# A decoder block on one core: gate and up by seven block products, their result through DRAM, down for eight output tiles at a time

## The chip, the cores and the metric

The kernel runs on one core of a Trainium2 chip. The metric is the device time of one execution in microseconds. Three runs of the kernel before took 2851.36 to 2853.41 us, with a median of 2852.76.

## The reference, cut to what matters

One hybrid block on 512 tokens of width 2048, in float32: an RWKV-7 branch and a spatial gating branch, merged by gates, an output projection with a residual add, then a SwiGLU channel mixer of hidden width 5632, and a final norm. The change lies in the channel mixer and the output projection ahead of it:

```
    h = h + merged @ w_out[l]
    n = _rmsnorm(h, norm_ffn_g[l])
    h = h + (jax.nn.silu(n @ w_ffn_gate[l]) * (n @ w_ffn_up[l])) @ w_ffn_down[l]
    return _rmsnorm(h, norm_final_g)
```

## The kernel before, in words

Everything is held transposed: a tile has 128 channels on its partitions and the 512 tokens beside each other. 2048 channels are 16 tiles (`KT`), the hidden width is 44 (`NHID`). The factor of the norm (`rs`, one number per token) is applied after the product, its gain before it.

**A product in three matmuls.** Each operand is split into a rounded part (`hi`, type float32r) and the rest (`lo`). `mm3` (L115 to L118) multiplies hi by hi, hi by lo and lo by hi into the same PSUM bank. Weights are the stationary operand, so each matmul comes with a weight load (LDWEIGHTS, engine PEld in the trace). `chunk` (L101 to L109) loads 512 KB of weights on SP's queue, ACT casts them to hi (L96), DVE subtracts to get lo (L99); three buffers of each stand in the pool `wp`. `block` (L133 to L138) computes two output tiles of 128 channels into the two banks of one of two `big` buffers.

**The stages.** Input projections with `nT` as moving tiles, kept in 32 tiles named "a" (L176 to L532); the RWKV chain beside them; the spatial gating (tiles "yb") and the two projections of the branches (tiles "yb" and "ya", L618 to L631), whose result `mg` takes the tiles "a" again; the output projection (L649 to L657), which adds the residual, multiplies by the gain g2 and splits into `n2`, in the tiles "a" too. The output projection's 16 tiles of `h` stay in `hA`.

**Gate, up and down.** `hidden` (L661 to L675) takes hidden tiles one by one: one `block` gives gate and up (2 x 16 x 3 = 96 matmuls of 512 columns), then DVE, ACT (silu), POOL and DVE build the hidden tile, and its two parts go into tiles "at". `down` (L677 to L682) multiplies a group of hidden tiles by their weights and adds to `hA`. The groups have 14, 14, 8, 4 and 4 tiles (L27); the last group's down is done for one half of the tokens and then for the other (`down_sq`, L700), 256 columns a matmul, with the final norm (`rms`, L155) and the stores between.

**Order.** The program is traced once and ordered by a planner, by priorities: what stands under `tc.high_priority()` (weight chunks, drains of PSUM) comes before what else is ready. Every engine then runs its list in that order, and so does SP's queue of DMAs.

**Where tiles lie.** Pools stack up from the left and from the right end of the 128-partition memory. The left one begins with 16 KB of DMA scratch and 8.3 KB of constants, so `wp` starts at byte 24704 of each partition and "a" behind it at 61568, both multiples of 128. The right end is 229344, 96 past a multiple of 128: "yb" and "ya" lie 96 past, the tiles "at", behind smaller ones of `fin`, 32 past.

## Time and profile before

| | |
|---|---|
| median of three runs | 2852.76 us |
| the profiled execution | 2852.42 us |
| its span, first to last instruction | 2850.7 us |
| granted TensorE clock over the span | 0.994 |
| PE busy, matmuls | 98%, 13968 |
| DVE busy | 48% |
| ACT busy | 29% |
| POOL busy | 8% |
| DMA, mean over the span | 121 GB/s |

PE is the matmul engine, PEld its weight loads, which overlap the matmuls; DVE, ACT and POOL work element by element, SP issues the DMAs. A matmul's recorded time includes the way through the array, so neighbours overlap, and the distance between starts tells its price. "Idle before" is the time in which an engine stood still ahead of an instruction, with what ended it.

### The profile page before, as it was taken

How to read it: one execution, taken by the hardware profiler on the slowest of the kernel's cores; microseconds unless marked ns; L12 is line 12 of the kernel's file. 1: busy time of each engine (PE TensorE's matmuls, PEld its weight loads, DVE VectorE, ACT ScalarE, POOL GpSimd, SP SyncE). 2: the span in 40 equal slices, each digit the busy share in tenths (PEclk: the TensorE clock that was granted, in tenths of full speed). 3: DMA queues.
4: the chain of work that ended last, by engine and by line, in shares of the span. 5: the costliest groups of instructions: out<-in, count | busy, mean ns of one | idle time of the engine just before them, and what ended most of it. 6: DMA issues, size and time to landing. Idle time of an engine off the chain costs nothing.

```text
span 2850.7 us, 33823 instructions
## 1 busy us (share of the span) xinstructions
PE 2795.5 (98%) x13968; PEld 2309.3 (81%) x13968; DVE 1359.1 (48%) x1508; ACT 832.5 (29%) x1050; POOL 230.0 (8%) x208
## 2 busy tenths in 40 slices
...
GB/s 161 123 150 155 155 193 117 103 109 104 252 213 120 173 123 136 143 153 96 96 96 96 96 96 89 103 96 96 96 96 90 95 103 97 90 99 98 98 92 152
DMA packets 172729, 345.94 MB, mean 121 GB/s; under 512 B 54304, under 2 KB 91168, under 8 KB 170272
## 3 DMA queue, kind: packets, MB, share of 16 engines
...
q8 instruction: 109, 1.79, 0.3%
...
HBM read 303.90 MB, written 39.85 MB: 121 GB/s over the span
## 4 chain that ended last, share of the span: by engine, by line
PE 85%; DVE 8%; issue 3%; DMA 2%; POOL 1%; SPq 0%; ACT 0%; POOLq 0%; DVEq 0%; ACTq 0%
PE ps_big L118 26%; PE ps_big L117 26%; PE ps_big L116 26%; DVE tmp L394 3%; DVE w_lo L99 2%; DVE X L396 2%; PE ps_big L528 1%; PE ps_big L527 1%; PE ps_big L526 1%; PE rkps L365 1%; DVE gt L512 0%; PE rkps L460 0%; POOL acc L646 0%; PE rkps L499 0%; DMA Ld<-d_l 0%
## 5 line engine op out<-in xcount | busy, mean ns | idle before, releaser
L118 PE MATMUL ps_big<-a,w_lo 128*128 128x512 f32 (+1 forms) x2752 | 1079.8, 393 | 28.0 <-DVE w_lo L99 27.9
L116 PE MATMUL ps_big<-a,w_hi 128*128 128x512 f32 (+1 forms) x2752 | 1077.3, 392 | 5.7 <-ACT w_hi L96 5.7
L117 PE MATMUL ps_big<-a,w_hi 128*128 128x512 f32 (+1 forms) x2752 | 1076.6, 391 | 0.0
L99 DVE TENSOR_TENSOR w_lo<-w_raw,w_hi 128x1024 fp32r<-128x1024 f32 (+2 forms) x500 | 608.9, 1219 | 929.0 <-ACT w_hi L96 924.0
L96 ACT CAST w_hi<-w_raw 128x1024 fp32r<-128x1024 f32 (+2 forms) x500 | 514.1, 1030 | 1497.0 <-PE ps_big L117 1441.6
L118 PEld LDWEIGHTS ps_big<-a,w_lo 128*128 128x128 f32 (+1 forms) x2752 | 518.5, 188 | 148.1 <-DVE w_lo L99 38.9
L116 PEld LDWEIGHTS ps_big<-a,w_hi 128*128 128x128 f32 (+1 forms) x2752 | 518.2, 188 | 114.8 <-ACT w_hi L96 5.7
L117 PEld LDWEIGHTS ps_big<-a,w_hi 128*128 128x128 f32 (+1 forms) x2752 | 518.4, 188 | 110.1 <-issue 0.2
L116 PE MATMUL ps_big<-at,w_hi 128*128 128x512 f32 (+1 forms) x768 | 288.6, 376 | 3.4 <-DVE hA L682 2.3
L118 PE MATMUL ps_big<-at,w_lo 128*128 128x512 f32 (+1 forms) x768 | 288.7, 376 | 0.0
L117 PE MATMUL ps_big<-at,w_hi 128*128 128x512 f32 (+1 forms) x768 | 288.4, 376 | 0.0
L668 POOL TENSOR_TENSOR sl<-sl,rs 128x512 f32<-128x512 f32 x44 | 78.5, 1785 | 1282.0 <-ACT sl L667 1282.0
L116 PEld LDWEIGHTS ps_big<-at,w_hi 128*128 128x128 f32 x768 | 144.0, 188 | 33.2 <-issue 2.5
L117 PEld LDWEIGHTS ps_big<-at,w_hi 128*128 128x128 f32 x768 | 144.0, 188 | 29.4
L118 PEld LDWEIGHTS ps_big<-at,w_lo 128*128 128x128 f32 x768 | 144.0, 188 | 29.3
L394 DVE TENSOR_TENSOR tmp<-X,Ld 128x1 f32<-128x1 f32 (+46 forms) x94 | 141.5, 1505 | 6.3 <-DMA Ld<-d_l 4.0
L666 DVE TENSOR_TENSOR sl<-ps_big,rs 128x512 f32<-128x512 f32 x44 | 30.4, 692 | 145.9 <-PE ps_big L118 145.9
L682 DVE TENSOR_TENSOR hA<-ps_big,hA 128x512 f32<-128x512 f32 (+1 forms) x96 | 53.3, 597 | 74.4 <-PE ps_big L118 74.4
L396 DVE TENSOR_REDUCE X<-tmp 128x1 f32<-128x1 f32 (+46 forms) x94 | 86.8, 923 | 2.3
L646 POOL TENSOR_TENSOR acc<-acc,sq 128x256 f32<-128x256 f32 (+1 forms) x41 | 52.1, 1271 | 433.4 <-ACT sq L645 385.4
L528 PE MATMUL ps_big<-w_hi,a 128*128 128x256 f32 x256 | 73.4, 287 | 0.0
L527 PE MATMUL ps_big<-w_lo,a 128*128 128x256 f32 x256 | 73.3, 286 | 0.0
...
## 6 DMA issues: line engine op xcount, KB each, us to landing
w_raw<-w_gu SPq DMA_DIRECT2D x176, 512.0 KB, 3.7
w_raw<-w_in SPq DMA_DIRECT2D x145, 512.0 KB, 3.7
w_raw<-w_dn SPq DMA_DIRECT2D x88, 512.0 KB, 3.6
...
w_raw<-w_out SPq DMA_DIRECT2D x32, 512.0 KB, 3.7
w_raw<-w_ps SPq DMA_DIRECT2D x16, 512.0 KB, 4.0
w_raw<-w_pr SPq DMA_DIRECT2D x16, 512.0 KB, 3.7
...
```

The source lines that it names most:

```text
L96: act.copy(out=dst, in_=src)
L99: (eng or dve).tensor_tensor(out=dst, in0=src, in1=hi.bitcast(F32), op=ALU.subtract)
L116: pe.matmul(out, wh, xh, start=start, stop=False)
L117: pe.matmul(out, wh, xl, start=False, stop=False)
L118: pe.matmul(out, wl, xh, start=False, stop=stop)
L394: dve.tensor_tensor(out=tv_, in0=X[:, s0:s1, s0:t], in1=Ld[:, s0:t, t].unsqueeze(1).to_broadcast([128, n, k]), op=ALU.mult)
L396: dve.tensor_reduce(out=X[:, s0:s1, t], in_=tv_, axis=AX.X, op=ALU.add)
L527: pe.matmul(o, nT[kk][0][:, ts], lo[:, k, :], start=False, stop=False, skip_group_check=True)
L528: pe.matmul(o, nT[kk][1][:, ts], hi[:, k, :], start=False, stop=kk == KT - 1, skip_group_check=True)
L646: pool.tensor_tensor(out=acc[:, sl], in0=acc[:, sl], in1=sq[:, sl], op=ALU.add)
L668: pool.tensor_tensor(out=sl, in0=sl, in1=rs, op=ALU.mult)
L682: dve.tensor_tensor(out=hT[j][:, ts], in0=ps[i], in1=hT[j][:, ts], op=ALU.add)
```

## The change

**The seven products.** The 16 channel tiles go by pairs: x1 is the even tile, x2 the odd one, each with its tokens in two halves T1 and T2. So the activation is a matrix of 2 x 2 blocks, and the weights of one hidden tile are four blocks of 8 x 128 rows by 128 columns: b11 (even channels, gate), b12 (even, up), b21 (odd, gate), b22 (odd, up). Winograd's form of Strassen's algorithm gives the four results (gate and up for each half of the tokens) from seven products, of b11, b21, b22 and four sums of blocks with x1[T1], x2[T1], x2[T2] and four sums S of halves. A product is 8 channel pairs x 3 matmuls of 256 columns, 168 a hidden tile.

**Activation side.** The output projection now also forms, pair by pair, the parts X1, X2 and XS (hi and lo each) and the sums S; its weights use two buffers of each kind (pool `wp2`); `h` goes to DRAM (`d_h`).

**Weight side.** For each hidden tile SP loads four blocks of 512 KB into six buffers; DVE forms four differences, ACT casts seven matrices, DVE subtracts seven low parts. Their buffers are two of each kind in each of two pools, taken in turn: four pairs in all.

**PSUM.** Three banks (A, B, Cb, with two buffers each) take the seven products; between two products into the same bank ACT copies it or DVE reads it. The hidden tile is stored to DRAM (`d_hid`), unsplit.

**Down.** For each half of the output (eight tiles, eight banks) a pass over 40 hidden tiles loads each from DRAM, splits it, loads and splits 1024 columns of its weights, and adds 24 matmuls of 512 columns. The last four hidden tiles are done as before, by halves of the tokens, with weight rows of 1 KB. `rms` takes its banks from the same eight.

**Where tiles lie now.** The DMA scratch is 1 KB. The left side's own constants, with an unused tile of 64 bytes (`PAD`), add up to 3936 bytes behind 1152, so `wp`, `wp2` and the X tiles begin at 5088 or whole multiples of 128 behind it: 96 past a multiple of 128. The tiles "a" are at the right end now, 96 past as well, with the other constants in padded sizes behind them, and so are the second pools of weights and the hidden tiles.

```diff
-PART_TILES = [14, 14, 8, 4, 4]
+MAIN = 40
...
-    wp = ctx.enter_context(tc.tile_pool(name="wp", bufs=3))
-    ap = ctx.enter_context(tc.tile_pool(name="ap", bufs=32))
-    big = ctx.enter_context(tc.tile_pool(name="big", bufs=2, space=PS))
-    rk = ctx.enter_context(tc.tile_pool(name="rk", bufs=4, space=PS))
+    lwp = ExitStack()
+    wp = lwp.enter_context(tc.tile_pool(name="wp", bufs=3))
+    rap = ExitStack()
+    ap = rap.enter_context(tc.tile_pool(name="ap", bufs=32, side="right"))
+    rcs = ExitStack()
+    csp = rcs.enter_context(tc.tile_pool(name="csp", bufs=1, side="right"))
+    psx = ExitStack()
+    big = psx.enter_context(tc.tile_pool(name="big", bufs=2, space=PS))
+    rk = psx.enter_context(tc.tile_pool(name="rk", bufs=4, space=PS))
...
+    const.tile([128, PAD], F32, name="pad")
+    cols = [const.tile([128, 2], F32, name=f"col{i}") for i in range(2)]
...
+    rcs.close()
+    lwp.close()
+    wp = ctx.enter_context(tc.tile_pool(name="wp2", bufs=2, reuse_waits="tile"))
+    lx = ExitStack()
+    xp = lx.enter_context(tc.tile_pool(name="xp", bufs=1))
+    X1 = [xp.tile([128, 8, 256], F32R, name=f"x1{q}") for q in "hl"]
+    X2 = [xp.tile([128, 8, 512], F32R, name=f"x2{q}") for q in "hl"]
+    XS = [xp.tile([128, 8, 4, 256], F32R, name=f"xs{q}") for q in "hl"]
+    T1, T2 = slice(0, 256), slice(256, 512)
+    def form_x(hi, lo, src):
+        hi_of(hi, src)
+        lo_of(lo, src, hi)
+    rh = ExitStack()
+    hp = rh.enter_context(tc.tile_pool(name="hp", bufs=1, side="right", reuse_waits="tile"))
+    acc = hp.tile([128, 512], F32, name="acc2")
+    for b in range(8):
+        ps = block(w_out[b], KT, mg)
+        xs = hp.tile([128, 2, 512], F32, name="xs2")
+        for i in range(2):
+            j = 2 * b + i
+            h = hp.tile([128, 512], F32, name="h", bufs=2)
+            nc.sync.dma_start(out=h, in_=xT[j])
+            with tc.high_priority():
+                dve.tensor_tensor(out=h, in0=ps[i], in1=h, op=ALU.add)
+                act.mul(xs[:, i, :], h, P("g2", j))
+            nc.sync.dma_start(out=d_h[j], in_=h)
+            if j == 0:
+                act.activation(out=acc, in_=h, func=AF.Square)
+            else:
+                sq = hp.tile([128, 512], F32, name="sq2")
+                act.activation(out=sq, in_=h, func=AF.Square)
+                pool.tensor_tensor(out=acc, in0=acc, in1=sq, op=ALU.add)
+        x1, x2 = xs[:, 0, :], xs[:, 1, :]
+        form_x(X1[0][:, b, :], X1[1][:, b, :], x1[:, T1])
+        form_x(X2[0][:, b, :], X2[1][:, b, :], x2)
+        S = hp.tile([128, 4, 256], F32, name="S")
+        dve.tensor_tensor(out=S[:, 0, :], in0=x1[:, T2], in1=x2[:, T2], op=ALU.add)
+        dve.tensor_tensor(out=S[:, 1, :], in0=S[:, 0, :], in1=x1[:, T1], op=ALU.subtract)
+        dve.tensor_tensor(out=S[:, 2, :], in0=x1[:, T1], in1=x1[:, T2], op=ALU.subtract)
+        dve.tensor_tensor(out=S[:, 3, :], in0=x2[:, T1], in1=S[:, 1, :], op=ALU.subtract)
+        form_x(XS[0][:, b], XS[1][:, b], S)
+    rms(acc, 4, rs_c, hp.tile([128, 512], F32, name="sq2"), rs)
+    rh.close()
+    rap.close()
+    psx.close()
+    pst = ExitStack()
...
+    gps = pst.enter_context(tc.tile_pool(name="gps", bufs=2, space=PS, reuse_waits="tile"))
+    rgu = ExitStack()
+    gp_ = rgu.enter_context(tc.tile_pool(name="gu", bufs=1, side="right", reuse_waits="tile"))
+    xA11 = [x[:, :, :] for x in X1]
+    xA12, xA22 = [x[:, :, T1] for x in X2], [x[:, :, T2] for x in X2]
+    xS1, xS2, xS3, xS4 = ([x[:, :, q, :] for x in XS] for q in range(4))
+    wn = [0]
+    def ring(name, dt):
+        p = (wp, gp_)[wn[0] % 2]
+        return p.tile([128, 8, 128], dt, name=name, tag=name, bufs=2)
+    def form_w(src):
+        hi, lo = ring("w_hi", F32R), ring("w_lo", F32R)
+        wn[0] += 1
+        hi_of(hi, src)
+        lo_of(lo, src, hi)
+        return hi, lo
+    def product(bank, w, x, first):
+        for k in range(8):
+            wh, wl, xh, xl = w[0][:, k, :], w[1][:, k, :], x[0][:, k, :], x[1][:, k, :]
+            pe.matmul(bank, wh, xh, start=first and k == 0, stop=False, skip_group_check=True)
+            pe.matmul(bank, wh, xl, start=False, stop=False, skip_group_check=True)
+            pe.matmul(bank, wl, xh, start=False, stop=k == 7, skip_group_check=True)
+    def sub(out, a, b):
+        dve.tensor_tensor(out=out, in0=a, in1=b, op=ALU.subtract)
+    def add(out, a, b):
+        dve.tensor_tensor(out=out, in0=a, in1=b, op=ALU.add)
+    for j in range(NHID):
+        with tc.high_priority():
+            b11, b12, b21, b22 = (gp_.tile([128, 8, 128], F32, name="wq", bufs=WQ) for q in range(4))
+            for q, t in enumerate((b11, b12, b22, b21)):
+                nc.sync.dma_start(out=t, in_=w_gu[j, (0, 1, 3, 2)[q]])
+            t1 = gp_.tile([128, 8, 128], F32, name="wt1")
+            t2 = gp_.tile([128, 8, 128], F32, name="wt2")
+            f11 = form_w(b11)
+            sub(t1, b12, b11)
+            sub(t2, b22, t1)
+            f2 = form_w(t2)
+            f21 = form_w(b21)
+            sub(b12, b22, b12)
+            f3 = form_w(b12)
+            f1 = form_w(t1)
+            sub(t2, b21, t2)
+            f4 = form_w(t2)
+            f22 = form_w(b22)
+        A, B, Cb = (gps.tile([128, 512], F32, name=n)[:, 0:256] for n in ("gA", "gB", "gC_"))
+        p1, u2, u3 = (gp_.tile([128, 256], F32, name=n, bufs=2) for n in ("p1", "u2", "u3"))
+        sl = gp_.tile([128, 512], F32, name="sl", bufs=2)
+        up = gp_.tile([128, 512], F32, name="up", bufs=2)
+        product(A, f11, xA11, True)
+        with tc.high_priority():
+            act.copy(out=p1, in_=A)
+        product(B, f2, xS2, True)
+        with tc.high_priority():
+            add(u2, B, p1)
+        product(A, f21, xA12, False)
+        with tc.high_priority():
+            dve.tensor_tensor(out=sl[:, T1], in0=A, in1=rs[:, T1], op=ALU.mult)
+        product(B, f3, xS3, False)
+        with tc.high_priority():
+            add(u3, B, p1)
+        product(Cb, f1, xS1, True)
+        with tc.high_priority():
+            add(up[:, T2], Cb, u3)
+        product(B, f4, xA22, False)
+        with tc.high_priority():
+            add(sl[:, T2], B, p1)
+            dve.tensor_tensor(out=sl[:, T2], in0=sl[:, T2], in1=rs[:, T2], op=ALU.mult)
+        product(Cb, f22, xS4, False)
+        with tc.high_priority():
+            add(up[:, T1], Cb, u2)
+        act.activation(out=sl, in_=sl, func=AF.Silu)
+        dve.tensor_tensor(out=up, in0=up, in1=rs, op=ALU.mult)
+        dve.tensor_tensor(out=sl, in0=sl, in1=up, op=ALU.mult)
+        nc.sync.dma_start(out=d_hid[j], in_=sl)
+    rgu.close()
+    lx.close()
+    pst.close()
+    dps = ctx.enter_context(tc.tile_pool(name="dps", bufs=8, space=PS, reuse_waits="tile"))
+    rk = dps
+    fin = ctx.enter_context(tc.tile_pool(name="fin", bufs=1, side="right", reuse_waits="tile"))
+    hA = ctx.enter_context(tc.tile_pool(name="hAp", bufs=1, reuse_waits="tile")).tile([128, KT, 512], F32, name="hA")
     hT = [hA[:, j, :] for j in range(KT)]
...
+    def hidden(k, bufs, tag):
+        raw = fin.tile([128, 512], F32, name="hraw", bufs=3)
+        nc.sync.dma_start(out=raw, in_=d_hid[k])
+        hi = fin.tile([128, 512], F32R, name=tag + "h", tag=tag + "h", bufs=bufs)
+        lo = fin.tile([128, 512], F32R, name=tag + "l", tag=tag + "l", bufs=bufs)
+        hi_of(hi, raw)
+        lo_of(lo, raw, hi)
+        return hi, lo
+    def down_w(src, n, w):
+        p = (wp, fin)[wn[0] % 2]
+        wn[0] += 1
+        raw = p.tile([128, n, w], F32, name="w_raw", tag="w_raw", bufs=2, padded_shape=[128, 1024 // w, w])
+        nc.sync.dma_start(out=raw, in_=src)
+        hi = p.tile([128, n, w], F32R, name="w_hi", tag="w_hi", bufs=2, padded_shape=[128, 1024 // w, w])
+        lo = p.tile([128, n, w], F32R, name="w_lo", tag="w_lo", bufs=2, padded_shape=[128, 1024 // w, w])
+        hi_of(hi, raw)
+        lo_of(lo, raw, hi)
+        return hi, lo
+    for q in range(2):
+        outs = [bank() for i in range(8)]
+        for k in range(MAIN):
+            with tc.high_priority():
+                xh, xl = hidden(k, 3, "x")
+                wh, wl = down_w(w_dn[q, k].unsqueeze(1), 1, 1024)
+            for i in range(8):
+                c = slice(128 * i, 128 * i + 128)
+                mm3(outs[i], wh[:, 0, c], wl[:, 0, c], xh, xl, k == 0, k == MAIN - 1)
+            if k == 8:
+                nc.sync.dma_start(out=hA[:, 8 * q:8 * q + 8], in_=d_h[8 * q:8 * q + 8].rearrange("k p t -> p k t"))
+        for i in range(8):
+            with tc.high_priority():
+                add(hT[8 * q + i], outs[i], hT[8 * q + i])
+    at2 = [hidden(k, NHID - MAIN, "z") for k in range(MAIN, NHID)]
...
+    def down_sq(b, ts):
+        n = NHID - MAIN
+        with tc.high_priority():
+            wh, wl = down_w(w_dn[b // 4, MAIN:NHID, :, 256 * (b % 4):256 * (b % 4) + 256].rearrange("k r c -> r k c"),
+                            n, 256)
+        res = []
         for i in range(2):
             j = 2 * b + i
+            ps = bank()[:, 0:256]
+            for k in range(n):
+                c = slice(128 * i, 128 * i + 128)
+                mm3(ps, wh[:, k, c], wl[:, k, c], at2[k][0][:, ts], at2[k][1][:, ts], k == 0, k == n - 1)
+            add(hT[j][:, ts], ps, hT[j][:, ts])
...
-    gu = np.stack([i["w_ffn_gate"][0].reshape(D, NHID, 128), i["w_ffn_up"][0].reshape(D, NHID, 128)], 2)
-    a["w_gu"] = _blocks(gu.reshape(D, 2 * HID))
-    a["w_dn"] = _blocks(i["w_ffn_down"][0])
+    gu = np.stack([i["w_ffn_gate"][0], i["w_ffn_up"][0]]).reshape(2, 8, 2, 128, NHID, 128)
+
+    a["w_gu"] = np.ascontiguousarray(gu.transpose(4, 2, 0, 3, 1, 5)).reshape(NHID, 4, 128, 8, 128)
+    a["w_dn"] = np.ascontiguousarray(i["w_ffn_down"][0].reshape(NHID, 128, 2, 1024).transpose(2, 0, 1, 3))
...
-    nc = _bacc.Bacc("TRN2", target_bir_lowering=False, num_devices=1)
+    nc = _bacc.Bacc("TRN2", target_bir_lowering=False, num_devices=1, dynamic_dma_scratch_size=1024)
```

## Rows read from the trace of the kernel before

**Rows 1.** The page: busy time by engine, and the chain that ended last.
```profile
PE 2795.5 (98%) x13968; PEld 2309.3 (81%) x13968; DVE 1359.1 (48%) x1508; ACT 832.5 (29%) x1050; POOL 230.0 (8%) x208
...
PE 85%; DVE 8%; issue 3%; DMA 2%; POOL 1%; SPq 0%; ACT 0%; POOLq 0%; DVEq 0%; ACTq 0%
PE ps_big L118 26%; PE ps_big L117 26%; PE ps_big L116 26%; DVE tmp L394 3%; DVE w_lo L99 2%; DVE X L396 2%; PE ps_big L528 1%; PE ps_big L527 1%; PE ps_big L526 1%; PE rkps L365 1%; DVE gt L512 0%; PE rkps L460 0%; POOL acc L646 0%; PE rkps L499 0%; DMA Ld<-d_l 0%
```

**Rows 2.** Stretches: PE, PEld, DVE, ACT, POOL busy us (instructions), clock, DMA share, GB/s.
```profile
1425.00:1500.00 75.00, 75.00 (x333) 62.12 (x332) 24.61 (x25) 18.17 (x22) 7.18 (x4) 1.00 0.32 98
2200.00:2275.00 75.00, 75.00 (x323) 60.22 (x323) 21.04 (x23) 14.04 (x15) 0.00 (x0) 1.00 0.34 99
...
1350.00:1425.00 75.00, 75.00 (x335) 61.88 (x334) 35.94 (x40) 32.48 (x41) 7.67 (x5) 1.00 0.31 96
750.00:825.00 75.00, 75.00 (x922) 67.32 (x922) 37.20 (x60) 29.55 (x50) 13.11 (x24) 1.00 0.65 219
```

**Rows 3.** Timeline of PE: start us, us, instruction; gate and up, 512 columns.
```profile
2734.91 0.39 PE L116 MATMUL ps_big<-a,w_hi 128*128 128x512 f32 x1
...
2740.35 0.39 PE L116 MATMUL ps_big<-a,w_hi 128*128 128x512 f32 x1
```

**Rows 4.** Timeline of PE: down, "at" moving, 512 columns.
```profile
2741.03 0.40 PE L116 MATMUL ps_big<-at,w_hi 128*128 128x512 f32 x1
...
2752.93 0.40 PE L116 MATMUL ps_big<-at,w_hi 128*128 128x512 f32 x1
```

**Rows 5.** Timeline of PE: SGU projection, "yb" moving, 512 columns.
```profile
1071.33 0.39 PE L116 MATMUL ps_big<-yb_hi,w_hi 128*128 128x512 f32 x1
...
1072.73 0.39 PE L116 MATMUL ps_big<-yb_hi,w_hi 128*128 128x512 f32 x1
```

**Rows 6.** Timeline of PE: the tail of down, 256 columns of "at" moving.
```profile
2787.95 0.28 PE L116 MATMUL ps_big<-at,w_hi 128*128 128x256 f32 x1
...
2797.85 0.28 PE L116 MATMUL ps_big<-at,w_hi 128*128 128x256 f32 x1
```

**Rows 7.** Timeline of PE: SGU input, 256 columns of a weight tile moving.
```profile
859.79 0.28 PE L526 MATMUL ps_big<-w_hi,a 128*128 128x256 f32 x1
...
866.27 0.28 PE L526 MATMUL ps_big<-w_hi,a 128*128 128x256 f32 x1
```

**Rows 8.** A group of weight loads: count, busy us, mean ns.
```profile
L526 PEld LDWEIGHTS ps_big<-w_hi,a 128*128 128x128 f32 x256 | 48.9, 191 | 0.6
```

**Rows 9.** Timeline of PE: RWKV gate, 512 columns, weights and moving at one offset.
```profile
943.10 0.39 PE L116 MATMUL rkps<-xg_hi,gwh 128*128 128x512 f32 x1
...
944.24 0.40 PE L118 MATMUL rkps<-xg_hi,gwl 128*128 128x512 f32 x1
```

**Rows 10.** Groups of DVE and ACT: line, shape, count, busy us, mean ns.
```profile
L99 DVE TENSOR_TENSOR w_lo<-w_raw,w_hi 128x1024 fp32r<-128x1024 f32 x473 | 584.8, 1237 | 871.5 <-ACT w_hi L96 866.5 <-DMA d_l<-SC 4.2 <-DMA d_c<-SC 0.8
L666 DVE TENSOR_TENSOR sl<-ps_big,rs 128x512 f32<-128x512 f32 x44 | 30.4, 692 | 145.9 <-PE ps_big L118 145.9
L682 DVE TENSOR_TENSOR hA<-ps_big,hA 128x256 f32<-128x256 f32 x32 | 12.1, 418 | 10.3 <-PE ps_big L118 10.3
...
L96 ACT CAST w_hi<-w_raw 128x1024 fp32r<-128x1024 f32 x473 | 497.1, 1053 | 1418.7 <-PE ps_big L117 1363.3 <-issue 29.1 <-PE ps_big L528 12.5
L151 ACT ACTIVATE a<-hA,par_t 128x512 fp32r<-128x512 f32 x16 | 11.3, 724 | 6.2 <-PE ps_big L117 6.2
```

**Rows 11.** Timeline of DVE: ops in a row, then the tail; idle in brackets.
```profile
1363.63 1.21 DVE L99 TENSOR_TENSOR w_lo<-w_raw,w_hi 128x1024 fp32r<-128x1024 f32 x1
1364.77 0.74 DVE L152 SCALAR_TENSOR_TENSOR a<-hA,par_t,a 128x512 fp32r<-128x512 f32 x1
...
2791.69 0.76 DVE L682 TENSOR_TENSOR hA<-ps_big,hA 128x256 f32<-128x256 f32 x2 [0.63 <-PE ps_big L118]
2792.66 1.23 DVE L99 TENSOR_TENSOR w_lo<-w_raw,w_hi 128x1024 fp32r<-128x1024 f32 x1 [0.22 <-ACT w_hi L96]
```

**Rows 12.** DMA issues: count, KB each, median us to landing.
```profile
w_raw<-w_gu SPq DMA_DIRECT2D x176, 512.0 KB, 3.7
```

More of the change, by code (lines that the diff above doesn't have):

```diff
@@ L72, in body @@
     d_gb = dram.tile([16, 128, 512], F32, name="d_gb")
+    d_h = dram.tile([16, 128, 512], F32, name="d_h")
+    d_hid = dram.tile([NHID, 128, 512], F32, name="d_hid")
     par_t = const.tile([128, NPAR], F32, name="par_t")
@@ L195, in body @@
             nc.sync.dma_start(out=cst_t, in_=cst)
+            nc.sync.dma_start(out=ident, in_=cst[:, 0:128])
         for k in range(k0, k0 + n):
@@ new lines, in body, with bank @@
+    rgu.close()
[5 more added lines that the diff above has]
+    hA = ctx.enter_context(tc.tile_pool(name="hAp", bufs=1, reuse_waits="tile")).tile([128, KT, 512], F32, name="hA")
+    hT = [hA[:, j, :] for j in range(KT)]
+    def bank(name="dk"):
+        return dps.tile([128, 512], F32, name="rkps", tag="rkps")
@@ L641, in sum_sq @@
+    at2 = [hidden(k, NHID - MAIN, "z") for k in range(MAIN, NHID)]
+    acc = fin.tile([128, 512], F32, name="acc3")
+    H0, H1 = T1, T2
+    rbs = rs[:, 0:256]
+    def sum_sq(j, sl):
         if j == 0:
@@ L646, in sum_sq @@
             pool.tensor_tensor(out=acc[:, sl], in0=acc[:, sl], in1=sq[:, sl], op=ALU.add)
-    n2 = []
-    for b in range(8):
-        ps = block(w_out[b], KT, mg)
+    def down_sq(b, ts):
[4 more added lines that the diff above has]
+        res = []
         for i in range(2):
             j = 2 * b + i
-            nc.sync.dma_start(out=hT[j], in_=xT[j])
-            with tc.high_priority():
-                dve.tensor_tensor(out=hT[j], in0=ps[i], in1=hT[j], op=ALU.add)
-                n2.append(scaled_split(hT[j], P("g2", j), ap, "a"))
-            sum_sq(j)
@@ L658, in body @@
-    rms(acc, 4, rs_c, fin.tile([128, 512], F32, name="sq2", bufs=2), rs)
-    def hidden(js):
-        res = []
-        for j in js:
-            ps = block(w_gu[j], KT, n2)
-            sl = fin.tile([128, 512], F32, name="sl", bufs=2)
-            dve.tensor_tensor(out=sl, in0=ps[0], in1=rs, op=ALU.mult)
-            act.activation(out=sl, in_=sl, func=AF.Silu)
-            pool.tensor_tensor(out=sl, in0=sl, in1=rs, op=ALU.mult)
-            dve.tensor_tensor(out=sl, in0=sl, in1=ps[1], op=ALU.mult)
-            hi = fin.tile([128, 512], F32R, name="at", tag="at", bufs=28)
-            lo = fin.tile([128, 512], F32R, name="at", tag="at", bufs=28)
-            hi_of(hi, sl)
-            lo_of(lo, sl, hi)
-            res.append((hi, lo))
-        return res
@@ L677, in down @@
-    def down(b, k0, ats, ts):
-        npt = len(ats)
-        ps = block(w_dn[b][:, k0:k0 + npt, :], npt, [(x[:, ts], y[:, ts]) for x, y in ats], n=ts.stop - ts.start)
-        for i in range(2):
-            j = 2 * b + i
-            dve.tensor_tensor(out=hT[j][:, ts], in0=ps[i], in1=hT[j][:, ts], op=ALU.add)
-    full = slice(0, 512)
-    h0 = 0
-    for npt in PART_TILES[:-2]:
-        ats = hidden(range(h0, h0 + npt))
-        for b in range(8):
-            down(b, h0, ats, full)
-        h0 += npt
@@ L691, in body @@
-    n1, n2_ = PART_TILES[-2:]
-    at1 = hidden(range(h0, h0 + n1))
-    at2 = hidden(range(h0 + n1, h0 + n1 + n2_))
-    for b in range(8):
-        down(b, h0, at1, full)
-    h0 += n1
-    H0, H1 = slice(0, 256), slice(256, 512)
-    rbs = rs[:, 0:256]
-    def down_sq(b, ts):
-        down(b, h0, at2, ts)
-        res = []
+            ps = bank()[:, 0:256]
+            for k in range(n):
+                c = slice(128 * i, 128 * i + 128)
+                mm3(ps, wh[:, k, c], wl[:, k, c], at2[k][0][:, ts], at2[k][1][:, ts], k == 0, k == n - 1)
@@ L726, in body @@
         sqs = down_sq(b, H0)
-    col = fin.tile([128, 2], F32, name="col", bufs=2)
-    dg = fin.tile([128, 512], F32, name="sl", bufs=2)
+    col = cols.pop()
+    dg = fin.tile([128, 512], F32, name="dg", bufs=2)
     rb = rms([acc[:, H0]] + sqs, 2, col, dg)
@@ L733, in body @@
         scale_out(b, H0, rbs, lambda k: k % 2 == 1)
[L734 to L735 removed]
+    col = cols.pop()
+    dg = fin.tile([128, 512], F32, name="dg", bufs=2)
     rb = rms([acc[:, H1]] + sqs, 2, col, dg)
```

16 lines of the change are left out of this document (6 added, 10 removed).

## Prediction

> **What bounds the kernel now.** I read the page's table of engines first, then the chain that ended last, then stretches of the feed-forward part, then single rows for prices. TensorE is busy 98% of the span, and the chain runs on it for 85%, nearly all of that in three lines, the triple of matmuls in mm3 [rows 1]. One can be misled here: a matmul's recorded duration (0.39 us) overlaps the next one's, so its price is the distance between starts. In a gate/up stretch and in a down stretch PE has no idle time at the full clock, DVE 25 and 21 us of work in 75, ACT 18 and 14, POOL 7 and 0, and the DMA moves 98 GB/s where another stretch shows 219 [rows 2]. So in this part only TensorE's own time counts, and a change is worth the pairs of weight load and matmul that it removes, less every wait that it brings into an engine that has none now.
>
> **Prices of one pair, start to start.** 512 columns with an "a" tile moving: (2740.35 - 2734.91) / 24 = 226.7 ns [rows 3]. 512 columns with an "at" tile: (2752.93 - 2741.03) / 51 = 233.3 ns [rows 4]; with "yb", (1072.73 - 1071.33) / 6 = 233.3 [rows 5]. 256 columns with "at": (2797.85 - 2787.95) / 84 = 117.9 [rows 6]; 256 columns with a weight tile moving and "a" as weights: (866.27 - 859.79) / 54 = 120.0 [rows 7]. Every one of these pairs has its own weight load.
>
> **Gate and up.** Now 44 tiles x 2 x 16 x 3 = 4224 matmuls of 512 columns: 957.6 us, 21.76 a tile. Afterwards 44 x 7 products x 8 x 3 = 7392 of 256 columns. Half the columns cost more than half the time (120.0 against 113.3), so of the eighth that the algorithm saves, part goes to the weight loads, whose number grows by three quarters. I take 120.0, the row in which both operands lie at the same offset, as they do after the change (next paragraph): 887.0 us, 20.16 a tile, **-70.6**. With 117.9 it is 871.5 (-86.1). The ends for an untried mix of operands are half of 226.7 (838, -120) and half of 233.3 plus the 6.7 by which 120.0 exceeds 113.3 (911, -47).
>
> The Trainium skill (TensorE: Matmul & The Clock Gate, "Measured speedup vs the span model") says that a weight load overlaps running matmuls only when it goes to another row group, and all of these go to the same. By that rule a pair would be load plus stream, and halving the stream would gain little. No such sum is seen here: a load is recorded with 191 ns [rows 8], yet pairs follow each other every 118 to 120 ns, so loads and streams do overlap. The same page ("Back-to-back issue gap") gives a sustained 81 ns at 128 columns and 131 at 512; an estimate between them (98 at 256) would make gate and up 7392 x 98 against 4224 x 131, 171 us slower. The trace has 226.7 and 120.0 instead, and it decides.
>
> **Where the tiles lie.** What tells 226.7 from 233.3 is not the shape. Weights and "a" start at multiples of 128 bytes, "at" 32 and "yb" 96 bytes past one. Where moving tile and weights are both 96 past, the rows settle at (944.24 - 943.10) / 5 = 228 [rows 9]. I read this as: equal offsets give 227, unequal ones 233. After the change all these tiles lie 96 past (sizes summed in the section on the change). Then down's 1920 matmuls go from 233.3 to 226.7, **-12.7**, those of the two projections (768) likewise, **-5.1**, and the 384 of the tail go from 117.9 to 120.0, **+0.8**. Bounds: no gain at all (0), or, if it is the multiple of 128 itself that counts, the 4032 pairs that have 226.7 today in the earlier stages go to 233.3, +26.6.
>
> **DVE and ACT beside the products.** A tile now gives DVE four differences and seven low parts of 1024 elements. One such op takes 1.24 us alone [rows 10] and 1.14 behind another (1364.77 - 1363.63) [rows 11]. With seven ops of 256 (0.42 alone, 0.34 in a row) and two of 512 (0.69, 0.6) that is 11 x 1.14 + 7 x 0.34 + 2 x 0.6 = 16.1 us, or 18.0 at full durations, for 20.16 us of PE: covered, at 80 to 89%. ACT has seven casts of 1.05, and a silu and a copy that are together no more than an eighth: 8.4 us. POOL loses its multiplication (it hid beside PE: nothing). SP loads four blocks of 512 KB a tile, as now, each landing in 3.7 us [rows 12], and gains a 256 KB store; 2.25 MB in 20 us is 112 GB/s. The store waits at SP's head for a tile's last op with the next loads behind it; six block buffers put those loads a product or more ahead.
>
> New are waits of PE: the three banks are read in between (bank A by ACT after the first product, B by DVE after the second and the fourth, C after the fifth), and the product after next writes the same bank. One product is 24 x 0.12 = 2.9 us. If DVE is in a large op when the product ends, the read is done after 1.14 + 0.42 + 0.2, that is 1.8 us: hidden. With two large ops queued ahead it takes 0.63 (a drain's wait in the tail, same rows) + 2.28 + 0.42 = 3.3, and 0.4 us shows. Four pairs of weight buffers let DVE run three products ahead. I take one such miss in three tiles or so, 0.15 us a tile, **+6.6**; bounds 0 and 1.0 a tile (44).
>
> **Seams.** Before the products: the last block's sum (0.69), multiplication by g2 (0.72), four sums of 256 (1.7), cast (1.05) and low part (1.23) make 5.4 us, before the second product's last eighth; PE meanwhile has the first product and seven eighths of the second, 2.9 + 2.5. But DVE must also make the first weights then (some four ops of 1.14), and its place for them comes free only as the last block is read. I take 3 us; PE idles for nothing there now (75.0 of 75) [rows 2]. Weight buffers go from three to two in the output projection; a chunk is 24 x 0.227 = 5.4 us, cast and low part take 2.3: nothing, 1 us where the pool moves. Into down: its first weights and hidden tiles lie in buffers that free before the last product: 1 us. Down itself: eight output tiles for each hidden one, 24 x 0.227 = 5.4 us, for 0.69 + 1.23 of DVE and 768 KB (141 GB/s): hidden; draining a bank (0.6) stays ahead of PE, which returns to it after seven others. Together **+5**, bounds 0 and 15.
>
> **Sum.** -70.6 - 12.7 - 5.1 + 0.8 + 6.6 + 5 = -76.0. The profiled execution took 2852.4 (span 2850.7, 1.7 around it), 0.3 below the median shown, so **2776**.
>
> **Rivals.**
> Offsets pay nothing: 2776 + 12.7 + 5.1 = 2794, and 2820 with the 26.6. For it: three groups of rows are all that I have, and the 96-past one is short. Chance 0.14.
> Waits eat a part: 0.5 to 1.7 us a tile in place of 0.15, 2791 to 2844. For it: DVE at 80 to 89% has little slack, and its queue is in a fixed order. Chance 0.12.
> Slower: banks and DVE lock each other. If three large ops stand before the read at two banks of a tile, each read ends 0.63 + 3.4 + 0.42 = 4.5 us after its product, 1.6 beyond the cover, 3.2 a tile: 2776 - 6.6 + 141 = 2910. It decides from 1.88 us a tile, (76.0 + 6.6) / 44. For it: a low part waits 0.2 for its cast and a drain 0.6 for its product in the tail [rows 11], so the chain is tight. Against it: the reads come earlier in the program than the next tile's weights, and are raised as those are. Chance 0.09.
> Loads bind: at the recorded 191 ns a pair, 7392 x 0.191 = 1412, 3301 in all. Rows 6 and 7 speak against it: 0.01. This is where the page's rule would lead.
>
> The forecast has 0.61, and 0.03 is left for a sum that comes out even. What can't be told from no change is 0.2%, 5.7 us: faster 0.86, same 0.04, slower 0.10. The forecast's own range is 2748 (117.9 ns and no waits: 2776 - 15.5 - 11.6) to 2791; with the offsets and the smaller waits I give 2748 to 2824.
>
> **What would show it.** Distance of the products' matmuls 120 (or 118) and a tile every 20.2 to 20.4 us; down's at 227; PE's waits for DVE or ACT in the product lines below 10 us in all; DVE near 80% there. Wrong: tiles 21 us or more apart with PE released by DVE (banks or low parts), or earlier stages at 233.

## The result, and the profile after

The changed kernel takes **2807.78 us** (median of four runs, 2807.22 to 2811.57), the one before, measured beside it, 2852.96: a ratio of 0.9845, 95% interval 0.9828 to 0.9863, 45 us less. Forecast were 2776 and a range of 2748 to 2824. So the sign and the range hold, and the gain is 45 us where 76 were worked out. The forecast's own range, 2748 to 2791, does not hold; the time lies in the part that was added for two rivals, and neither of them came (the section on why the prediction was right says more). The profiled execution took 2808.28 us, its span 2806.6.

The page's line of engines for the changed kernel, to [rows 1]: DVE has gone from 48% to 66%, PE from 98% to 97%.

```profile
PE 2719.2 (97%) x17136; PEld 2412.7 (86%) x17136; DVE 1849.1 (66%) x2148; ACT 1014.9 (36%) x1282; POOL 149.5 (5%) x164
```

Stretches of 75 us of the changed kernel, columns as in [rows 2]: the products (1425), down (2325), and two stretches in which a stage gives way to the next (1350, 2250).

```profile
1350.00:1425.00 75.00, 60.50 (x364) 54.04 (x363) 47.73 (x55) 30.59 (x38) 5.42 (x4) 0.89 0.47 150
1425.00:1500.00 75.00, 75.00 (x627) 75.00 (x626) 62.56 (x76) 30.29 (x34) 0.00 (x0) 1.00 0.37 111
...
2250.00:2325.00 75.00, 57.72 (x384) 53.47 (x383) 36.24 (x45) 21.72 (x25) 0.00 (x0) 0.89 0.44 149
2325.00:2400.00 75.00, 75.00 (x333) 62.10 (x332) 25.52 (x28) 22.03 (x28) 0.00 (x0) 1.00 0.45 146
```

In the products and in down PE has no idle time. In the two stretches around the products it loses 14.5 and 17.3 us, and the mean clock falls to 0.89. The timeline of PE in the changed kernel shows where, and what a pair costs:

```profile
1023.79 0.48 PE L125 MATMUL ps_big<-yb_hi,w_hi 128*128 128x512 f32 x1
...
1197.74 0.39 PE L127 MATMUL ps_big<-ya,w_lo 128*128 128x512 f32 x1
1201.70 0.80 PE L125 MATMUL ps_big<-a,w_hi 128*128 128x512 f32 x1 [3.58 <-ACT w_hi L105]
...
1378.72 0.39 PE L127 MATMUL ps_big<-a,w_lo 128*128 128x512 f32 x1
1386.32 1.87 PE L171 MATMUL rkps<-ones,acc 128*128 128x1 f32 x8 [7.21 <-POOL acc L682]
1395.48 2.07 PE L179 MATMUL rkps<-sq,ones 128*128 128x512 f32 x2 [7.29 <-DVE sq L175]
1396.57 1.20 PE L721 MATMUL gA<-x1h,w_hi 128*128 128x256 f32 x1
...
1501.72 0.28 PE L721 MATMUL gB<-xsh,w_hi 128*128 128x256 f32 x1
...
1521.88 0.28 PE L721 MATMUL gB<-xsh,w_hi 128*128 128x256 f32 x1
...
2284.96 0.28 PE L723 MATMUL gC__20665<-xsh,w_lo 128*128 128x256 f32 x1
2302.51 3.78 PE L125 MATMUL rkps<-xh,w_hi 128*128 128x512 f32 x8 [17.28 <-ACT xh L105]
2306.10 0.63 PE L126 MATMUL rkps<-xl,w_hi 128*128 128x512 f32 x1
...
2499.62 0.39 PE L127 MATMUL rkps<-xh,w_lo 128*128 128x512 f32 x1
...
2506.42 0.39 PE L127 MATMUL rkps<-xh,w_lo 128*128 128x512 f32 x1
...
2739.89 0.28 PE L125 MATMUL rkps<-zh,w_hi 128*128 128x256 f32 x1
```

A hidden tile takes 1521.88 - 1501.72 = 20.16 us, 168 pairs of 120.0 ns. In down (2506.42 - 2499.62) / 30 = 226.7 ns. The same view of the kernel before has the borders of its stages:

```profile
1025.03 0.48 PE L116 MATMUL ps_big<-yb_hi,w_hi 128*128 128x512 f32 x1
...
1204.33 0.40 PE L116 MATMUL ps_big<-a,w_hi 128*128 128x512 f32 x1
...
2785.83 0.28 PE L116 MATMUL ps_big<-at,w_hi 128*128 128x256 f32 x1
```

From these starts the whole difference of the two spans (2850.7 - 2806.6 = 44.1) can be laid out. One pair is added to the last start of a stage to get its end.

| stretch | how | us |
|---|---|---|
| ahead of the projections | 1023.79 - 1025.03 | -1.2 |
| projections | (1197.97 - 1023.79) - (1204.33 - 1025.03) | -5.1 |
| gap before the output projection | 1201.70 - 1197.97 | +3.7 |
| output projection | (1378.95 - 1201.70) - 768 x 0.2267 | +3.1 |
| gap before the products | 1396.57 - 1378.95 | +17.6 |
| products | 887.0 - 957.6 (pairs of 0.120 and 0.2267) | -70.6 |
| above 0.120 in them | (2285.08 - 1396.57) - 887.0 | +1.5 |
| gap before down | 2302.51 - 2285.08 | +17.4 |
| down | 1920 x (0.2267 - 0.2333) | -12.7 |
| above 0.2267 in it | (2739.89 - 2302.51) - 435.3 | +2.1 |
| tail | (2806.6 - 2739.89) - (2850.7 - 2785.83) | +1.8 |
| before: gate, up and down above their pairs | 1405.5 - (2785.83 - 1204.33 - 174.1) | -1.9 |
| sum | | -44.3 |

So the three seams cost 3.7 + 3.1 + 17.6 + 1.5 + 17.4 + 2.1 = **45.4 us**. Of these 38.7 are PE standing still or doing only the norm's few matmuls, and 6.7 are what the first matmuls behind each stop take above their usual price. Down's first eight are (2306.10 - 2302.51) / 8 = 449 ns apart in place of 227; the granted clock between these two starts is 0.50, the lower of the two levels, 1.2 in place of 2.4 GHz. It is 0.50 from 1202 to 1206 and 0.51 from 1396.57 to 1399, behind the other two stops.

What PE waited for before the products is in the rows above: POOL's sum of squares, then DVE's diagonal tile for the norm's broadcast (L175). PE runs its list in order, so the norm, which nothing needs before the first tile's third product is read, held up the products behind it. DVE's timeline of the changed kernel shows why L175 was late: it stands in DVE's list behind a row of large ops for the first weights and the last X parts, and DVE has no gap there. SP's timeline shows the first weight blocks issued only when the output projection's last matmul had been reached, since their buffers lie where the "a" tiles lay; and, before down, 4 MB of `h` and the last store ahead of the first hidden tile.

```profile
1392.51 1.18 DVE L108 TENSOR_TENSOR w_lo<-wt,w_hi 128x1024 fp32r<-128x1024 f32 x1
1393.62 1.21 DVE L108 TENSOR_TENSOR w_lo<-wq,w_hi 128x1024 fp32r<-128x1024 f32 x1
1394.75 0.68 DVE L175 TENSOR_TENSOR sq<-ident,rs_c 128x512 f32<-128x512 f32 x1
```

```profile
1379.14 2.80 SPq L735 DMA_DIRECT2D wq<-w_gu  x6
...
2285.05 1.00 SPq L823 DMA_DIRECT2D hA<-d_h  x2
2287.25 4.43 SPq L778 DMA_DIRECT2D d_hid<-sl  x1
2291.74 1.79 SPq L795 DMA_DIRECT2D hraw<-d_hid  x3
```

### The profile page after: what moved, and what is told of

Its sections match the earlier page's. It is cut to its first block, busy times and chain, and to the rows that moved or that the text cites. A ratio compares the mean times of both kernels' runs of the same rounds, so it can differ in the third digit from the quotient of the medians.

```text
span 2806.6 us, 41671 instructions
## 1 busy us (share of the span) xinstructions
PE 2719.2 (97%) x17136; PEld 2412.7 (86%) x17136; DVE 1849.1 (66%) x2148; ACT 1014.9 (36%) x1282; POOL 149.5 (5%) x164
## 4 chain that ended last, share of the span: by engine, by line
PE 87%; DVE 7%; issue 3%; DMA 1%; POOL 0%; ACT 0%; SPq 0%; POOLq 0%; DVEq 0%; ACTq 0%
PE ps_big L127 10%; PE ps_big L125 10%; PE ps_big L126 10%; PE rkps L125 6%; PE rkps L126 6%; PE rkps L127 6%; PE gB L722 5%; PE gB L721 5%; PE gB L723 5%; PE gA L721 3%; PE gA L722 3%; PE gA L723 3%; DVE tmp L406 2%; DVE w_lo L108 2%; DVE X L408 1%
## 5 line engine op out<-in xcount | busy, mean ns | idle before, releaser
L108 DVE TENSOR_TENSOR w_lo<-w_raw,w_hi 128x1024 fp32r<-128x1024 f32 (+2 forms) x316 | 391.3, 1239 | 502.8 <-ACT w_hi L105 502.6
L127 PE MATMUL ps_big<-a,w_lo 128*128 128x512 f32 (+1 forms) x1344 | 533.5, 397 | 26.9 <-DVE w_lo L108 26.9
L125 PE MATMUL ps_big<-a,w_hi 128*128 128x512 f32 (+1 forms) x1344 | 530.8, 395 | 8.8 <-ACT w_hi L105 8.8
L126 PE MATMUL ps_big<-a,w_hi 128*128 128x512 f32 (+1 forms) x1344 | 529.6, 394 | 0.2 <-DVE a L161 0.2
L127 PEld LDWEIGHTS ps_big<-a,w_lo 128*128 128x128 f32 (+1 forms) x1344 | 254.6, 189 | 93.9 <-DVE w_lo L108 39.1
L125 PEld LDWEIGHTS ps_big<-a,w_hi 128*128 128x128 f32 (+1 forms) x1344 | 254.8, 190 | 63.0 <-ACT w_hi L105 9.2
L126 PEld LDWEIGHTS ps_big<-a,w_hi 128*128 128x128 f32 (+1 forms) x1344 | 255.0, 190 | 55.8 <-DVE a L161 0.7
L125 PE MATMUL rkps<-xh,w_hi 128*128 128x512 f32 x640 | 249.5, 392 | 17.3 <-ACT xh L105 17.3
L126 PE MATMUL rkps<-xl,w_hi 128*128 128x512 f32 x640 | 249.2, 389 | 0.0
L127 PE MATMUL rkps<-xh,w_lo 128*128 128x512 f32 x640 | 249.0, 389 | 0.0
L108 DVE TENSOR_TENSOR w_lo<-wq,w_hi 128x1024 fp32r<-128x1024 f32 x176 | 215.0, 1221 | 26.1 <-ACT w_hi L105 23.6
L721 PE MATMUL gB<-xsh,w_hi 128*128 128x256 f32 x704 | 199.2, 283 | 0.0
```

The lines of the kernel that those rows point to most:

```text
L108: (eng or dve).tensor_tensor(out=dst, in0=src, in1=hi.bitcast(F32), op=ALU.subtract)
L125: pe.matmul(out, wh, xh, start=start, stop=False)
L126: pe.matmul(out, wh, xl, start=False, stop=False)
L127: pe.matmul(out, wl, xh, start=False, stop=stop)
L721: pe.matmul(bank, wh, xh, start=first and k == 0, stop=False, skip_group_check=True)
```

## The experiments

Each kernel is the changed one with the edit shown. Theory: the prices per pair are right, and the lost 31 us lie in the seams. Each run was timed beside the kernel before, whose median was 2851.0 to 2853.0. The differences given are to the 2807.78 of the changed kernel, so one of 2 us or less says nothing.

### The activation's tiles shifted by 32 bytes

```diff
+    xp.tile([128, 8], F32, name="xpad")
     X1 = [xp.tile([128, 8, 256], F32R, name=f"x1{q}") for q in "hl"]
```

> Edit: 32 unused bytes ahead of the X tiles, so that they start at a multiple of 128 bytes while all weights stay 96 past one. Theory of the offsets: pairs of 256 columns take 120.0 ns where both operands lie at one offset and 117.9 where they don't; 7392 x 2.1 = 15.5 us less, 2792, with product matmuls 117 to 118 ns apart. Rival: 120.0 and 117.9 differ for another reason (what moves, or which PSUM tile is written): no change, 2808.

Measured: 2784.32 us, ratio 0.9767 (0.9752 to 0.9781), 23.5 less than the changed kernel. The direction is the theory's, the size is larger. PE's timeline of this kernel: (1501.82 - 1500.07) / 15 = 116.7 ns a pair, for 120.0 before; 7392 x 3.3 = 24.

```profile
1500.07 0.28 PE L722 MATMUL gB<-xsh,w_hi 128*128 128x256 f32 x1
...
1501.82 0.28 PE L722 MATMUL gB<-xsh,w_hi 128*128 128x256 f32 x1
```

### Everything on the left shifted by 32 bytes

```diff
-PAD = 16
+PAD = 24
```

> Edit: the unused tile of 64 bytes is 96 bytes, so that all pools at the left (first pool of weights, X) start at a multiple of 128 bytes, while all at the right (tiles a, yb, ya, second pool of weights, hidden tiles) stay 96 past. Theory of the offsets: 512-column pairs with unequal offsets take 233.3 in place of 226.7: 4032 + 768 + half of down's 1920, that is +38; half of the products' pairs (weights at the right, X at the left) go from 120.0 to 117.9, -7.8, and the 256-column pairs of the gating -1.6: about +28, 2836. Rival 1: multiples of 128 are what makes a pair fast: the products and half of down gain nothing and lose nothing, earlier stages unchanged, 2808. Rival 2: the offset has no influence: 2808.

Measured: 2819.23, ratio 0.9887 (0.9872 to 0.9902), 11.5 more. In PE's timeline of this kernel the output projection's pairs ("a" on the right, weights on the left) are (1303.97 - 1299.78) / 18 = 232.8 ns apart. Of two neighbouring products one has its weights on the left, at the offset of X, the other on the right: 2.52 / 21 = 120.0 and 1.40 / 12 = 116.7.

```profile
1299.78 0.40 PE L125 MATMUL ps_big<-a,w_hi 128*128 128x512 f32 x1
...
1303.97 0.40 PE L125 MATMUL ps_big<-a,w_hi 128*128 128x512 f32 x1
...
1499.80 0.28 PE L721 MATMUL gB<-xsh,w_hi 128*128 128x256 f32 x1
...
1501.20 0.28 PE L721 MATMUL gB<-xsh,w_hi 128*128 128x256 f32 x1
...
1501.79 0.28 PE L721 MATMUL gA<-x2h,w_hi 128*128 128x256 f32 x1
...
1504.31 0.28 PE L721 MATMUL gA<-x2h,w_hi 128*128 128x256 f32 x1
```

This tells equal offsets from multiples of 128: both at a multiple gives 120.0, as both 96 past does in the changed kernel, and unequal ones 116.7. At 512 columns it is the other way round, 226.7 for equal and about 233 for unequal. The time is 17 us below the theory's 2836. The products gave 12 us (half of them 3.3 ns cheaper) where 7.8 were counted; that is 4.4 of the 17. Most of the rest is missing ahead of the products: the first one starts 18.2 us later than in the changed kernel (1414.79 against 1396.57), where 4800 x 6.6 ns, less 1.6, had made it 30. The pairs there do stand 233 ns apart; where these 12 us went was not settled.

### The norm behind the first tile's third product

```diff
-    rms(acc, 4, rs_c, hp.tile([128, 512], F32, name="sq2"), rs)
...
         product(A, f21, xA12, False)
+        if j == 0:
+            rms(acc, 4, rs_c, up, rs)
```

(with two PSUM banks of its own, and its sum in the pool of the X tiles)

> Edit: the norm's matmuls ahead of gate and up (rms) stand behind the third product of the first tile in place of ahead of the first, with two PSUM banks of their own. Theory: in the changed kernel PE's list holds the norm's matmuls before the first product; they wait for POOL's sum (7.2 us) and for DVE's diagonal, which is queued behind six large weight ops (7.3 us). Moved, the first product waits only for its own weights and the first product's inputs, some 1385.5 in place of 1396.6: about -9 us, 2799. Rival: the first tile's weights are what is late (their loads land at 1382.8 and DVE needs eight large ops for two pairs): -2 us at most, 2806.

Measured: 2801.93, ratio 0.9829 (0.9812 to 0.9845), 5.9 less: between theory and rival, and both hold a part. In PE's timeline of this kernel the first product starts 12 us earlier, at 1384.47, but it waits for its first weights, and the next ones for theirs; the granted clock from 1384.4 to 1388 is 0.50.

```profile
1384.47 0.58 PE L723 MATMUL gA<-x1h,w_hi 128*128 128x256 f32 x1 [4.91 <-ACT w_hi L105]
...
1391.91 0.38 PE L723 MATMUL gB<-xsh,w_hi 128*128 128x256 f32 x1 [1.03 <-ACT w_hi L105]
```

### The residual's 4 MB behind the first hidden tiles

```diff
             if k == 8:
-                nc.sync.dma_start(out=hA[:, 8 * q:8 * q + 8], ...)
+                with tc.issue_after(last_raw[0]):
+                    nc.sync.dma_start(out=hA[:, 8 * q:8 * q + 8], ...)
```

(`last_raw[0]` is the load of the hidden tile k = 8)

> Edit: the two loads of the residual (2 MB each) are queued on SP behind the load of the hidden tile k = 8, where the program has them. Theory: in the changed kernel these 4 MB stand ahead of the first hidden tiles in the DMA queues, which land 10 us after their issue in place of 3.7; without them down begins some 8 to 10 us earlier: 2798 to 2800. Rival: what is late is the last hidden tile's way through DRAM, since the loads are issued only behind its store: no change, 2806 to 2808.

Measured: 2798.09, ratio 0.9814 (0.9799 to 0.9829), 9.7 less, as the theory had it. PE's waits in this kernel (line waited for: us, times, longest): 5.9 us in place of 17.3. The 4 MB had cost twice: the first hidden tile's load is issued 2.7 us behind the start of the products' last matmul (2288.65 against 2285.99), in the changed kernel 6.8 (2291.74 against 2284.96, with the store ahead of it standing 4.43 us on SP), and it then landed late. What remains is the last tile's own work, its store, and the load behind it.

```profile
PE rkps L125 <- ACT xh L105: 5.9, 1, 5.9
```

### Two pairs of weight buffers in place of four

```diff
-        p = (wp, gp_)[wn[0] % 2]
+        p = wp
```

> Two pairs of weight buffers in place of four, nothing else. Theory (the lead of three products is what hides DVE's queue from TensorE): with two pairs a product's cast and low part (1.05 + 1.23 = 2.3 us) must fall within the one product of 2.9 us before it, together with the differences and the bank reads of DVE's queue; some 0.3 us a product show, 44 x 7 x 0.3 = +92, 2900 (2850 to 2960). Rival (no lead is needed, DVE at 84% keeps up by itself): 2808, 5 either way.

Measured: 2826.00, ratio 0.9910 (0.9895 to 0.9925), 18 more; neither number was met. In PE's timeline of this kernel one product in a tile, f4's, starts its third matmul 0.3 us late, when it needs the low part, and the next one 0.1: 44 x 0.4 = 18. DVE's subtraction for that low part starts at 1515.31 and takes 1.22 us; two differences and a read of a bank stand ahead of it. So the lead is needed, but for one product in seven. The planner's order changed too: here the seven products stand one behind the other, where the changed kernel has parts of them mixed, so the 18 us hold for the lead and that order together.

```profile
1516.15 0.28 PE L722 MATMUL gB<-x2l,w_hi 128*128 128x256 f32 x1
1516.58 0.39 PE L723 MATMUL gB<-x2h,w_lo 128*128 128x256 f32 x1
1516.80 0.28 PE L721 MATMUL gB<-x2h,w_hi 128*128 128x256 f32 x1
```

### More work for DVE: four ops a tile, then two

```diff
             f22 = form_w(b22)
+            for _ in range(4):      # 2 in the other kernel
+                sub(t1, b21, b22)
```

> Four more DVE differences of 1024 elements in each hidden tile, whose result nobody reads. DVE is busy 62 to 64 us in 75 in the products, 16.9 us a tile; with 4 x 1.14 more it is 21.4 for TensorE's 20.15. Theory (TensorE waits only when DVE as a whole is the longer): 44 x 1.25 = +55, 2863 (2850 to 2880), tiles every 21.4 us. Rival (reads of the banks stand behind large ops, so that each added one shows on TensorE, as in the forecast's slower case): 44 x 4.56 = +200, 3008, or at least over 2900.

Measured: 2862.16, ratio 1.0038 (1.0024 to 1.0053), 54 more, the theory's number.

> Two more DVE differences of 1024 elements in each hidden tile, whose result nobody reads. Theory (TensorE waits only when DVE's whole work is the longer, as with four more, which cost 54 us): 16.9 + 2 x 1.14 = 19.2 us a tile for TensorE's 20.15, so nothing, 2808 (2805 to 2812). Rival (four more cost what they cost because each stands before a read of a bank): half of it, 2835.

Measured: 2856.19 (2854.65 to 2863.36; the profiled execution is the longest), ratio 1.0018 (1.0007 to 1.0029), 48 more. **Here the theory falls**, and the rival misses too: two ops cost nearly what four cost, though DVE is far from full. A stretch of the kernel with four and the same of that with two (first and second fence):

```profile
2100.00:2175.00 75.00, 72.22 (x591) 71.41 (x592) 72.96 (x85) 29.34 (x34) 0.00 (x0) 1.00 0.34 117
```

```profile
2100.00:2175.00 75.00, 72.06 (x594) 71.25 (x594) 65.37 (x78) 28.55 (x33) 0.00 (x0) 1.00 0.37 109
```

DVE is busy 73.0 of 75 us with four and 65.4 with two, and PE loses 2.8 and 2.9. PE's timeline with two shows the place:

```profile
1560.19 0.38 PE L721 MATMUL gA<-x1h,w_hi 128*128 128x256 f32 x1 [1.02 <-ACT w_hi L105]
...
1561.13 0.38 PE L721 MATMUL gB<-xsh,w_hi 128*128 128x256 f32 x1 [0.45 <-ACT w_hi L105]
...
1561.47 0.28 PE L721 MATMUL gB<-x2h,w_hi 128*128 128x256 f32 x1
```

The planner has put the first two matmuls of the next tile's first two products ahead of f4's product of this tile (gB<-x2h), and f3's product just ahead of them. The cast for the first of them waits for PE itself, with 4.66 us idle on ACT, because its buffer is that of f3:

```profile
1559.09 1.04 ACT L105 CAST w_hi<-wq 128x1024 fp32r<-128x1024 f32 x1 [4.66 <-PE gB L722]
```

PE waits for these two casts 20 and 21 times, 30 us in all (line waited for: us, times, longest; first fence). From one such place to the next, two tiles on, it is 1602.49 - 1560.19 = 42.30 us in place of 40.32, and 1646.28 - 1602.49 = 43.79 where the clock fell after the wait (granted 0.97 from 1600 to 1700). With four ops (second fence) PE waits for the first cast 21 times, and ahead of another product 22 times, 15.8 us in all; two tiles take 1543.44 - 1500.62 = 42.82 us.

```profile
PE gA L721 <- ACT w_hi L105: 20.4, 20, 1.0
PE gB L721 <- ACT w_hi L105: 9.8, 21, 0.8
```

```profile
PE gA L721 <- ACT w_hi L105: 21.4, 21, 1.0
```

42.82 us are the theory's 21.4 a tile, and DVE is busy 97% there, so the run with four cannot tell whether DVE's sum or the order sets its time. The run with two can: DVE has room, and the waits are there all the same. What DVE could take on without cost, were the order kept, stays open; no run has the added ops in the old order.

### The three helpful edits together, and with early loads

> The three single edits together: the norm's factor behind the third product, the residual's 4 MB behind the first hidden tiles of down, and the activation's tiles shifted by 32 bytes. Theory (three independent places on TensorE's path, so the sizes add): 2807.8 - 5.9 - 9.7 - 23.5 = 2769, 2 either way. Rival (what is saved at one seam is given back at the next, since DVE or the DMA is late there too): 2775 to 2784.

Measured: 2766.75, ratio 0.9706 (0.9692 to 0.9720). The theory's 2769: the sizes add.

```diff
+            if j == 0:    # b11, b12 in the output projection's load buffers
+                b11, b12 = (wp.tile([128, 8, 128], F32, name="w_raw", tag="w_raw") for q in range(2))
...
+        if j == 0:
+            product(Cb, f1, xS1, True)
         product(B, f2, xS2, True)
...
+        if j == 4:        # down's first hidden tile, into a tile of its own
+            nc.sync.dma_start(out=raw0, in_=d_hid[0])
```

> As the three together, and two more edits: the first tile's blocks b11 and b12 come in the output projection's own load buffers and f1's product stands second in that tile; the first hidden tile of down is loaded into a place of its own while the products still run. Theory (what is left of the seams is late first weights and a late first hidden tile): some 3 to 4 us less at each seam, 2762; TensorE idle before down under 3 us, in place of 5.9. Rival (DVE's row of a dozen large ops at the first products is what is late, whatever is loaded when): no gain there, 2766; at the worst the reordered tile costs what it gains, 2769.

Measured: 2763.27, ratio 0.9691 (0.9677 to 0.9706), 3.5 less than with three, which lies within the scatter of those runs (2764.70 to 2773.25). The traces show little gain: from the output projection's last matmul to the products' last one it is 874.8 us for 876.1, and from there to the tail 443.2 for 443.8. The products now start at once, and PE then waits 3.6 us for DVE's low part of the last X tile, as the rival had it. PE also starts down without the hidden tile's wait, and stands still before the second one, for that one's weights. PE's waits in this kernel:

```profile
PE rkps L125 <- ACT w_hi L105: 4.8, 1, 4.8
```

So the second weights were given a buffer on the left too:

```diff
-        p = (wp, fin)[wn[0] % 2]
+        p = (wp, wp, fin, fin)[dn[0]] if dn[0] < 4 else (wp, fin)[dn[0] % 2]
```

> As the kernel with five edits (2763.3), and down's second weights too into a buffer on the left, which is free while the products still run. Theory (TensorE stood still 4.8 us before down's second hidden tile, because its weights went to memory that the products held to the end): 2763.3 - 4.5 = 2759, 1 either way. Rival (the wait moves on to the third weights or to a hidden tile, since all loads of that moment share the DMA): 2762 to 2764.

Measured: 2763.86 (2757.87 to 2767.37), ratio 0.9689 (0.9675 to 0.9704). The seam is gone in PE's timeline of this kernel, whose products, the last one started at 2252.52, go over into down with one wait of 0.69 us. From the products' last matmul to the tail it is now 436.5 us for 443.2, so the theory's step is there, 6.6 us; the median does not show it, for its runs lie 9.5 us apart (the merge's section has two executions that differ by 8). That the median meets the rival's number is chance.

```profile
2252.64 2.11 PE L125 MATMUL rkps<-xh,w_hi 128*128 128x512 f32 x8
2255.44 0.50 PE L126 MATMUL rkps<-xl,w_hi 128*128 128x512 f32 x1 [0.69 <-DVE xl L108]
```

### The merge's order

```diff
             rps = block(w_pr[b], 8, ya)
+            if b == 7:
+                ... # wp closed, wp2 opened
+                with tc.high_priority():
+                    early = [chunk(w_out[0], k0, 4, 256) for k0 in (0, 4)]
```

> The changed kernel with one edit: the output projection's first two weight chunks stand in the program ahead of the merge's last two tiles, so that ACT's list has their casts first. Theory (TensorE stood still 3.96 us there and came back at half clock for another 3, because the first cast stood behind the last merge's): 2807.8 - 6 = 2802, 1 either way. Rival (the buffers come free no earlier, whatever the order): 2807 to 2809; if SP's queue is held by these loads, some us slower.

Measured: 2809.41, ratio 0.9852 (0.9836 to 0.9869), no gain. It did not try the theory: the planner kept its order. In ACT's timeline of this kernel the weight's cast still stands behind the merge's, 17.37 us idle ahead of both:

```profile
1201.10 0.62 ACT L105 CAST a<-ga_t 128x512 fp32r<-128x512 f32 x1 [17.37 <-DVE ga_t L647]
1201.62 1.04 ACT L105 CAST w_hi<-w_raw 128x1024 fp32r<-128x1024 f32 x1
```

> All seven edits: the two norm and residual moves, the shift of 32 bytes, first weights and first two loads of down early, and the merge's order. Theory (each is a wait of TensorE of its own, so the sizes add): 2763.3 - 4.5 - 6 = 2753, 2 either way, nearly all of it TensorE's own time. Rival (a saved wait comes back at the next seam): 2757 to 2763.

Measured: 2763.15 (2759.46 to 2768.50), ratio 0.9690 (0.9676 to 0.9705). That is the rival's number, but not for its reason: the merge's edit does nothing, and the seam into down stays saved (436.6 us from the products' last matmul to the tail). The profiled executions of the kernel without that edit (2757.87) and of this one (2765.44) differ in the products' pairs, (1502.94 - 1499.79) / 27 = 116.7 ns in the first and (1502.91 - 1499.73) / 27 = 117.8 in PE's timeline of the second, shown here; 7392 x 1.1 = 8 us, the whole difference. The distance is the same all through the products of each of the two. What sets it was not found.

```profile
1499.73 0.28 PE L733 MATMUL gB<-xsh,w_hi 128*128 128x256 f32 x1
...
1502.91 0.28 PE L735 MATMUL gC__11935<-xsh,w_lo 128*128 128x256 f32 x1
```

## Why the prediction was right, and where it was not

**Gate and up, -70.6: right to the row.** 120.0 ns a pair, from a stage with another shape of data but the same 256 columns and equal offsets [rows 7]. The rule of the Trainium skill weighed there (TensorE: Matmul & The Clock Gate; it stands in the section "The mechanism", not in the one that the prediction names) would have a pair cost load plus stream; the products' weight loads are recorded with 192 ns and their pairs start 120.0 apart, so here too they overlap.

**Where the tiles lie, -12.7 and -5.1: right.** Down has 226.7, the projections got shorter by 5.1. The reading of [rows 3 to 5, 9], equal against unequal offsets, is borne out by the two shifts. One chance was missed: I saw that unequal offsets make a 256-column pair cheaper (117.9 against 120.0 [rows 6, 7]) and priced it as a bound, -15.5; 32 bytes in the right place are worth 23.5.

**Waits of PE at the banks, +6.6: they are 0.** No wait of PE in the products stands in the trace, and PE is busy 75.0 of 75. DVE's work came out near the forecast (62 of 75 us, 83%, for 80 to 89%). But the reason given for the cover, spare time of DVE and a lead of three products, is only half of it. Two more ops in DVE's list, within its spare time, cost 48 us: in the lists that the planner then wrote PE waits for a cast of ACT, and ACT for a buffer that PE has only just read. The forecast's slower case spoke of such a lock, at the banks; it came at the weight buffers.

**Seams, +5 (bounds 0 and 15): this is the step that failed.** They cost 45. "I take 3 us" before the products counted DVE's ops for the last block, and left out the norm, two visits of PE in program order, and the row of some ten large ops behind which its diagonal stood; that the first blocks' place "comes free only as the last block is read" was seen and not priced. "Its first weights and hidden tiles lie in buffers that free before the last product" was wrong: only the weights of the first do. The first hidden tile's load stands on SP behind the last tile's store and goes into a pool that opens when the products' pool closes, and 4 MB of `h` were issued ahead of it. That took 17.4 us in place of 1. And no term stood for what follows a stop: 6.7 us of matmuls at the lower clock. The two moves take back 5.9 and 9.7. The loads brought forward take back another 7.2 us of the stretch from the products' last matmul to the tail (443.8 to 436.5 in the traces); the medians, whose runs scatter by as much, do not show it.

**Tail, +0.8:** it is +1.8, within what the stages around it scatter.

The sum was thus 31 us off by one term of 40 and a smaller one of -6.6, less 2 us in stretches that had no term; the rivals had no case for the seams, and their bound of 15 was where the range was too sure.

**The range held by luck.** The forecast's own range ended at 2791, and 2807.78 is 17 above. The end of 2824 was given for offsets that pay nothing and for waits at the banks. The offsets paid in full and the waits were 0; what the seams cost too much happened to fall into the room left for them. The rival "waits eat a part" has the measured time between its 2791 and 2844 too, and its place was equally wrong.
